# The first block of attention values on other PSUM banks and in other weight tiles, and a Newton step with one tensor operand

## The chip, the cores and the metric

The kernel runs on one NeuronCore of a Trainium2 chip. The metric is the device time of one execution in microseconds (us), as the median of several runs. Engines are named as in the profile: PE is TensorE's matmul, PEld its weight load, DVE is VectorE, ACT is ScalarE, POOL is GpSimd, SP is SyncE, which here only issues DMAs.

## What is computed

One step of a one-layer hybrid decoder: 1024 prompt rows and 8 sample rows of width 1024, everything in float32. The input is normalised, projected by one wide matrix, and goes through three branches (A is attention), which a second matrix merges:

```python
def _rms(x, g):
    xf = x.astype(F32)
    y = xf * lax.rsqrt(jnp.mean(xf * xf, axis=-1, keepdims=True) + EPS)
    return (y * g.astype(F32)).astype(x.dtype)
...
    h = _rms(x, norm_g)
    proj = jnp.einsum('bld,dn->bln', h, w_in)
    ...
    aq = _rms(aq.reshape(B, L, H_A, HD_A), qn_g.reshape(H_A, HD_A)) * (HD_A ** -0.5)
    ak = _rms(ak.reshape(B, L, H_A, HD_A), kn_g.reshape(H_A, HD_A))
    av = av.reshape(B, L, H_A, HD_A)
```

A has 12 heads of width 64 over a mixture of three dilated windows; B is a spatial gating unit, C a gated linear recurrence. The change touches the norm `_rms(x, norm_g)` of the input and the projection `av` of the first four heads.

## The kernel before

The prompt is cut into eight tiles of 128 rows (t = 0 to 7); the 8 sample rows are tile 8. A tile is loaded (`xt`), ACT squares it and sums the squares (`ss`), `rstd` turns the sum into 1/sqrt (a logarithm and an exponential on ACT, then one Newton step on DVE), DVE scales the rows (`xn`), for tiles 3 to 7 POOL multiplies by `norm_g` (2.4 us each), and PE transposes `xn` into PSUM. The result is split into a high and a low half (`h` by ACT, `h` by DVE), and each later product of 128 rows is three matmuls: high by high, high by low, low by high. `hs` holds the transposed sample rows.

`load_w` loads a block of 256 columns of the input matrix as four raw tiles (`wr`, six buffers), rounds each into `wh` (ACT) and takes the rest into `wl` (POOL), four buffers each. Block `qk0` is queries and keys of the first two heads, `v0` values of the first four, `az0` their gates. The four `wh` buffers of `qk0` are free for the next block only when its last product is done.

PSUM has eight banks: `p_proj` two, `p_st` four (scores, and at the start the transposes of `xn`), `p_tr` one, `p_pv` one. `qk_proj` fills the two `p_proj` banks in turn: `pss_qk` (sample rows), then `pqk` 0 to 3, each two row tiles. A `pqk` bank comes free only when ACT has squared it, DVE has summed the squares and made the Newton step, and DVE has written `nat` from it. `v_proj` goes on in the same two banks: `pss_v`, then `pv` 0 to 3. PE transposes `nat` (line 399) into `p_tr`, from where ACT and DVE make the operands of the scores (`KK`, `QQ`, ...).

Attention then works on one head after the other, named by pair and head: scores for the row maximum (`s`), scores again (`st`), exponentials, products with the values (`pv`), and at the end of each half a division, for which `pb` broadcasts the denominators. While PE would wait for ACT and DVE here, projections of later blocks are put between.

The order of all instructions on each engine is made at build time by a scheduler that goes through the program with costs of its own. A small edit can so move rows on every engine. Each engine and each DMA queue then goes through its list in order.

Of the kernel before, what the change touches and what calls it, by code (L numbers as in the profile page):

```python
# [9 lines left out]
F32R = mybir.dt.float32r  # L10
BF16 = mybir.dt.bfloat16
U8 = mybir.dt.uint8
AF = mybir.ActivationFunctionType
ALU = mybir.AluOpType
# [4 lines left out]
P = 128  # L19
D = 1024  # L20
KD = D // P
S = 1024
NT = S // P
# [3 lines left out]
NW = 256  # L27
# [4 lines left out]
EPS = 1e-6  # L32
WB = 2048
OFF_Q, OFF_K, OFF_V, OFF_AZ = 0, 768, 1536, 2304
# [8 lines left out]
N_BIG, N_S2, N_S2B, N_PQ, N_W, N_WL, N_GT, N_RAW, N_E = 16, 6, 2, 5, 4, 4, 2, 6, 3  # L43
# [48 lines left out]
def hybrid_step(tc, ins, outs, parts=("A", "D", "B", "C", "O"), dbg=None):  # L92
    nc = tc.nc
# [8 lines left out]
    with tc.tile_pool(name="const", bufs=1) as cp, tc.tile_pool(name="sb", bufs=1) as sb, \  # L102
            tc.tile_pool(name="ps", bufs=1, space=PSUM) as pm:

        def wk(nm, shape=(P, L), dt=F32):
            return sb.tile(list(shape), dt, tag="big", name=nm, bufs=N_BIG)

        def inp(nm, shape=(P, L), dt=F32):
            return sb.tile(list(shape), dt, tag="big", name=nm, bufs=N_BIG)

        def s2(nm, dt=F32, shape=(P, 512)):
            return sb.tile(list(shape), dt, tag="s2", name=nm, bufs=N_S2)

        def ee(nm, shape=(P, 512), dt=F32):
            return sb.tile(list(shape), dt, tag="e", name=nm, bufs=N_E)
# [4 lines left out]
        def pq(nm, shape=(P, 512), dt=F32):  # L120
            return sb.tile(list(shape), dt, tag="pq", name=nm, bufs=N_PQ)

        def small(nm, n, p=P, dt=F32, bufs=2, tag=None):
            return sb.tile([p, n], dt, tag=tag or f"sm{n}", name=nm, bufs=bufs)

        def psum(tag, nm, bufs, n=512):
            return pm.tile([P, n], F32, tag=tag, name=nm, bufs=bufs)

        def p_proj(nm):
            return psum("proj", nm, 2)  # L130
# [4 lines left out]
        def p_st(nm):  # L135
            return psum("st", nm, 4)
# [21 lines left out]
        def rstd(out, ss, scale, tmp, t2):  # L158

            nc.vector.tensor_scalar(tmp, ss, scale, EPS, ALU.mult, ALU.add)  # L160
            nc.scalar.activation(out, tmp, AF.Ln)
            nc.scalar.activation(out, out, AF.Exp, scale=-0.5)
            nc.vector.tensor_tensor(t2, out, out, ALU.mult)
            nc.vector.scalar_tensor_tensor(tmp, tmp, -0.5, t2, ALU.mult, ALU.mult)
            nc.vector.scalar_tensor_tensor(out, tmp, 1.5, out, ALU.add, ALU.mult)  # L165

        ident = cp.tile([P, P], F32, name="ident")
        nc.scalar.dma_start(ident, ins["ident"])
        ones = cp.tile([P, P], F32, name="ones")
# [9 lines left out]
        qkv_d = tc.dram_tile([4, NS, HA * E], F32, name="qkv_scr")  # L179


        def load_w(cols, nm):
            blk = []
            for i in range(KD // 2):
                hi = sb.tile([P, 2, NW], F32R, tag="whi", name=f"wh_{nm}_{i}", bufs=N_W)
                lo = sb.tile([P, 2, NW], F32R, tag="wlo", name=f"wl_{nm}_{i}", bufs=N_WL)
                raw = sb.tile([P, 2, NW], F32, tag="raw", name=f"wr_{nm}_{i}", bufs=N_RAW)
                o = 0
                for c, w in cols:
                    nc.sync.dma_start(raw[:, :, o:o + w], w_in[:, 2 * i:2 * i + 2, c:c + w])  # L190
                    o += w
                nc.scalar.copy(hi, raw)
                nc.gpsimd.tensor_tensor(lo, raw, hi.bitcast(F32), ALU.subtract)  # L193
                blk.append((hi, lo, raw))
            return blk
# [10 lines left out]
        for t in (0, NT, *range(1, NT)):  # L206
            n = P if t < NT else NS
            xt = inp(f"xt{t}", (P, D))
            nc.sync.dma_start(xt[:n, :], x_p[t * P:(t + 1) * P, :] if t < NT else x_s)
            if t == 1:  # L210
                blk_first = load_w([(OFF_Q, P), (OFF_K, P)], "qk0")
            xn = wk(f"xn{t}", (P, D))
            ss = small(f"ss{t}", 4)
            if t == NT:
                nc.vector.tensor_tensor_reduce(out=xn[:n, :], in0=xt[:n, :], in1=xt[:n, :], op0=ALU.mult, op1=ALU.add,
                                               scale=1.0, scalar=0.0, accum_out=ss[:n, 0:1])
            else:
                nc.scalar.activation(xn, xt, AF.Square, accum_out=ss[:, 0:1])
            rstd(ss[:n, 1:2], ss[:n, 0:1], 1.0 / D, ss[:n, 2:3], ss[:n, 3:4])
            if t in (0, 1, 2, NT):  # L220
                for c in (slice(0, 512), slice(512, D)):
                    nc.vector.scalar_tensor_tensor(xn[:n, c], xt[:n, c], ss[:n, 1:2], g_bc[:n, c], ALU.mult, ALU.mult)
            else:
                nc.vector.tensor_scalar(xn, xt, ss[:, 1:2], None, ALU.mult)
                nc.gpsimd.tensor_tensor(xn, xn, g_bc, ALU.mult)
            for j in range(2):
                ps = p_st(f"tr0_{t}_{j}").rearrange("p (a b) -> p a b", a=4)
                for i in range(4):
                    k = 4 * j + i
                    nc.tensor.transpose(ps[:, i, :n], xn[:n, k * P:(k + 1) * P], ident[:n, :n])  # L230
                hi = h_t[0][j][:, :, t * P:t * P + n]
                lo = h_t[1][j][:, :, t * P:t * P + n]
                nc.scalar.copy(hi, ps[:, :, :n])  # L233
                nc.vector.tensor_tensor(lo, ps[:, :, :n], hi.bitcast(F32), ALU.subtract)
                if t == NT:
                    nc.vector.tensor_copy(hs[:, 4 * j:4 * j + 4, :], ps[:, :, :n])

        def wsl(blk, k, a, b):
            hi, lo, _ = blk[k // 2]
            return hi[:, k % 2, a:b], lo[:, k % 2, a:b]  # L240
# [9 lines left out]
        def rows8(ps, K, i0=0, n=None):  # L250

            n = n or len(K)
            for i, (rows, w) in enumerate(K, i0):
                g = 32 * (i % 4)
                mm(ps[g:g + NS, :NW], rows, w, i < 4, i >= n - 4)

        def add_groups(dst, ps):
            nc.scalar.copy(dst, ps[32:32 + NS, :NW])
            for g in (64, 96, 0):
                nc.vector.tensor_tensor(dst, ps[g:g + NS, :NW], dst, ALU.add)  # L260

        def proj_nat_s(blk, nm):
            ps = p_proj(f"pss_{nm}")
            rows8(ps, [(hs[:, k, :], blk[k // 2][2][:, k % 2, :]) for k in range(KD)])
            dst = small(f"sd_{nm}", NW, NS, tag="sdst")
            add_groups(dst, ps)
            return dst
# [60 lines left out]
        def s_out(n):  # L328
            return outs[n][0, :, 0].rearrange("b h e -> b (h e)")

        VW = 2 * (E + 1)

        def v_proj(sp):
            blk = load_w([(OFF_V + sp * NW, NW)], f"v{sp}")
            st = proj_nat_s(blk, f"v{sp}")
            V = []
            for j in range(2):
                vh = inp(f"vh{sp}_{j}", (P, NT, VW), F32R)
                vl = inp(f"vl{sp}_{j}", (P, NT, P), F32R)
                nc.gpsimd.memset(vh.rearrange("p t (h e) -> p t h e", h=2)[:, :, :, E].bitcast(F32), 1.0)  # L340
                V.append((vh, vl))
            for g in range(4):
                ps = p_proj(f"pv{sp}_{g}").rearrange("p (a b) -> p a b", a=2)
                for j in range(2):
                    proj_nat(blk, 2 * g + j, ps[:, j, :])
                vr = pq(f"vr{sp}_{g}", (P, 2, NW))
                nc.scalar.copy(vr, ps)
                nc.sync.dma_start(new_v[2 * g * P:(2 * g + 2) * P, sp * NW:(sp + 1) * NW]
                                  .rearrange("(a q) c -> q a c", q=P), vr)
                if g < 2:  # L350
                    nc.sync.dma_start(v_d[2 * g * P:(2 * g + 2) * P, sp * NW:(sp + 1) * NW]
                                      .rearrange("(a q) c -> q a c", q=P), vr)
                for j in range(2):
                    vh, vl = V[j]
                    t2 = slice(2 * g, 2 * g + 2)
                    hi = vh[:, t2, :].rearrange("p a (h e) -> p a h e", h=2)[:, :, :, 0:E]
                    src = vr[:, :, j * P:(j + 1) * P].rearrange("p a (h e) -> p a h e", h=2)
                    nc.scalar.copy(hi, src)
                    nc.gpsimd.tensor_tensor(vl[:, t2, :].rearrange("p a (h e) -> p a h e", h=2), src,
                                            hi.bitcast(F32), ALU.subtract)  # L360
            nc.sync.dma_start(qkv_d[2, :, sp * NW:(sp + 1) * NW], st)
            nc.sync.dma_start(s_out("o_vs")[:, sp * NW:(sp + 1) * NW], st)
            return V
# [698 lines left out]
```

## Time and profile before

| | |
|---|---|
| time, median of 3 runs | 1364.37 us (1363.49 to 1366.2) |
| the profiled execution: its time, its span | 1367.91 us, 1366.1 us |
| PE busy | 1277.9 us, 94% of the span |
| DVE, ACT, POOL busy | 914.3, 661.0, 292.6 us |
| mean granted TensorE clock | 0.951 of full |

The span runs from the first instruction to the last of one execution. [...]

### The profile page before, as it was taken

The numbers are of one execution on the slowest core, as the hardware profiler recorded it, in microseconds if no ns is written. First come the engines' busy times: TensorE is split into PE (matmuls) and PEld (weight loads), VectorE is DVE, ScalarE is ACT, GpSimd is POOL, SyncE is SP. The second block draws the span as 40 slices with busy tenths as digits, with TensorE's granted clock in tenths as the row PEclk, the third lists the DMA queues.
The fourth block names the chain that finished last, engine by engine and source line by source line (L and its number), as shares of the span: only waits on it lengthen the run. The fifth ranks groups of instructions, "written<-read, shape, count | busy, mean of one in ns | idle before, by whom it ended". The sixth has DMA issues, their size and how long they took to land. (4 is left out here: it accounts for less than half of the span.)

```text
span 1366.1 us, 27783 instructions
## 1 busy us (share of the span) xinstructions
PE 1277.9 (94%) x10634; PEld 1160.8 (85%) x10634; DVE 914.3 (67%) x2439; ACT 661.0 (48%) x1510; POOL 292.6 (21%) x267
## 2 busy tenths in 40 slices
PE   4799999999889999999999998998899999999999
PEld 3699798779779797898888888987788899899998
DVE  5835775565774656668888988888887623654653
ACT  4435454454443554456654744545544423544543
POOL 2531210131121212112202020211111135311221
PEclk9899899889999799999999999999999999999999
DMA  6241122220221212202433243434253313612210
GB/s 220 42 141 36 47 66 70 59 68 18 58 84 58 76 36 77 65 29 67 119 97 109 90 121 115 111 97 134 61 156 96 92 32 108 207 51 81 74 46 31
DMA packets 165044, 114.23 MB, mean 84 GB/s; under 512 B 13944, under 2 KB 158864, under 8 KB 164912
## 3 DMA queue, kind: packets, MB, share of 16 engines
q1 hardware_dynamic: 157520, 110.28, 27.3%
q10 hardware_dynamic: 6816, 1.54, 0.5%
q8 instruction: 83, 1.36, 0.4%
q0 software_dynamic: 576, 0.64, 0.3%
q14 instruction: 49, 0.40, 0.1%
HBM read 84.60 MB, written 22.09 MB: 78 GB/s over the span
## 5 line engine op out<-in xcount | busy, mean ns | idle before, releaser
L100 PE MATMUL pqk<-wh_qk,h 128*128 128x256 f32 x768 | 159.6, 299 | 5.2 <-ACT h L233 2.8
L100 PE MATMUL pc<-h,wh_cqf 128*128 128x344 f32 x576 | 144.1, 332 | 4.5 <-DVE cz L152 4.5
L100 PE MATMUL po<-woh,yl 128*128 128x256 f32 x512 | 145.0, 284 | 1.9 <-POOL yl L1011 1.9
L100 PE MATMUL po<-woh,yh 128*128 128x256 f32 x512 | 145.7, 285 | 0.0
L100 PE MATMUL po<-wol,yh 128*128 128x256 f32 x512 | 144.4, 282 | 0.0
L100 PEld LDWEIGHTS pqk<-wh_qk,h 128*128 128x128 f32 x768 | 131.5, 204 | 9.8 <-ACT h L233 3.0
L100 PE MATMUL pqk<-wl_qk,h 128*128 128x256 f32 x384 | 114.0, 297 | 0.0
L100 PEld LDWEIGHTS pc<-h,wh_cqf 128*128 128x128 f32 x576 | 102.1, 194 | 7.1 <-DVE cz L152 5.0
L100 PEld LDWEIGHTS po<-woh,yh 128*128 128x128 f32 x512 | 97.1, 190 | 5.6 <-ACT yh L1010 3.9
L100 PEld LDWEIGHTS po<-woh,yl 128*128 128x128 f32 x512 | 97.2, 190 | 4.1 <-POOL yl L1011 2.4
L100 PEld LDWEIGHTS po<-wol,yh 128*128 128x128 f32 x512 | 97.3, 190 | 0.0
L100 PE MATMUL pc<-h,wl_cqf 128*128 128x344 f32 x288 | 94.9, 332 | 2.5 <-POOL wl_cqf L193 2.2
L436 DVE CUSTOM_DVE_ANT_0 s<-s,masks 128x512 f32<-128x512 f32 (+2 forms) x144 | 77.7, 584 | 13.8 <-PE s L100 13.3
L100 PE MATMUL pi<-wh_ci,h 128*128 128x256 f32 x384 | 77.6, 297 | 4.8 <-DVE dsc L925 1.9
L100 PE MATMUL pv<-wh_v,h 128*128 128x256 f32 x384 | 79.1, 297 | 1.9 <-DVE ss L165 1.6
L473 ACT ACTIVATE st<-st 128x512 f32<-128x512 f32 (+2 forms) x84 | 44.2, 536 | 72.9 <-PE st L100 70.2
L100 PEld LDWEIGHTS pqk<-wl_qk,h 128*128 128x128 f32 x384 | 78.1, 204 | 0.5
L100 PE MATMUL pcz<-h,wh_cz 128*128 128x344 f32 x288 | 71.5, 326 | 0.3 <-DVE q L152 0.3
L100 PE MATMUL paz<-h,wh_az 128*128 128x344 f32 x288 | 71.1, 329 | 0.0
L100 PEld LDWEIGHTS pi<-wh_ci,h 128*128 128x128 f32 x384 | 64.2, 201 | 6.9 <-issue 2.9
L1011 DVE TENSOR_TENSOR yl<-yb,yh 128x512 fp32r<-128x512 f32 x44 | 30.4, 692 | 58.0 <-ACT yh L1010 58.0
L100 PEld LDWEIGHTS pv<-wh_v,h 128*128 128x128 f32 x384 | 65.7, 204 | 3.0 <-ACT yo L499 1.8
(376 smaller groups left out, 3665.1 us busy)
## 6 DMA issues: line engine op xcount, KB each, us to landing
wro<-in_w_out_dram SPq DMA_DIRECT2D x32, 256.0 KB
wr_qk<-in_w_in_dram SPq DMA_DIRECT2D x48, 128.0 KB
wr_cqf<-in_w_in_dram SPq DMA_DIRECT2D x48, 128.0 KB
dk<-in_cache_k_dram SPq DMA_DIRECT2D x24, 192.0 KB
dv<-in_cache_v_dram SPq DMA_DIRECT2D x24, 192.0 KB
xt<-in_x_prompt_dram SPq DMA_DIRECT2D x8, 512.0 KB
xr<-in_x_prompt_dram SPq DMA_DIRECT2D x32, 128.0 KB
out_o_yp_dram<-xr SPq DMA_DIRECT2D x32, 128.0 KB
```

The source lines that it names most:

```text
L100: nc.tensor.matmul(out, lhsT=lhsT, rhs=rhs, start=start, stop=stop)
L436: nc.vector.tensor_tensor_reduce(out=ps[:, :w], in0=ps[:, :w], in1=nmask[:, S - n + c:S - n + c + w], op0=ALU.add, op1=ALU.max, scale=1.0, ...
L473: nc.scalar.activation(st[:, :o], st[:, :o], AF.Exp)
L1011: (nc.gpsimd if piece == 0 else nc.vector).tensor_tensor(yl[:, sl, :], y, yh[:, sl, :].bitcast(F32), ALU.subtract)
```

## The change

It has three parts. The values' block `v0` is loaded ahead of the projections into tiles that lie idle until the attention (`s2`, `e`), so it no longer waits for the buffers of `qk0`. Its products go to the four `p_st` banks. And the norm of the input takes `rstd_rows`, which has the same steps as `rstd` with instructions that read one tensor and per-row scalars, and tile 8's squares move from DVE to ACT.

```diff
+        def rstd_rows(out, ss, scale, tmp, t2):
+            nc.vector.tensor_scalar(tmp, ss, scale, EPS, ALU.mult, ALU.add)
+            nc.scalar.activation(out, tmp, AF.Ln)
+            nc.scalar.activation(out, out, AF.Exp, scale=-0.5)
+            nc.vector.tensor_scalar(t2, out, out, tmp, ALU.mult, ALU.mult)
+            nc.vector.tensor_scalar(t2, t2, -0.5, 1.5, ALU.mult, ALU.add)
+            nc.vector.tensor_scalar(out, t2, out, None, ALU.mult)
...
-        def load_w(cols, nm):
+        def load_w(cols, nm, spare=False):
...
+                if spare:
+                    hi = s2(f"wh_{nm}_{i}", F32R, (P, 2, NW))
+                    lo = s2(f"wl_{nm}_{i}", F32R, (P, 2, NW)) if i < 2 else ee(f"wl_{nm}_{i}", (P, 2, NW), F32R)
...
-            if t == NT:
-                nc.vector.tensor_tensor_reduce(out=xn[:n, :], in0=xt[:n, :], in1=xt[:n, :], op0=ALU.mult, op1=ALU.add,
-                                               scale=1.0, scalar=0.0, accum_out=ss[:n, 0:1])
-            else:
-                nc.scalar.activation(xn, xt, AF.Square, accum_out=ss[:, 0:1])
-            rstd(ss[:n, 1:2], ss[:n, 0:1], 1.0 / D, ss[:n, 2:3], ss[:n, 3:4])
+            nc.scalar.activation(xn[:n, :], xt[:n, :], AF.Square, accum_out=ss[:n, 0:1])
+            rstd_rows(ss[:n, 1:2], ss[:n, 0:1], 1.0 / D, ss[:n, 2:3], ss[:n, 3:4])
...
+        blk_v = load_w([(OFF_V, NW)], "v0", True)
...
-            ps = p_proj(f"pss_{nm}")
+            ps = (bank or p_proj)(f"pss_{nm}")
...
-            blk = load_w([(OFF_V + sp * NW, NW)], f"v{sp}")
-            st = proj_nat_s(blk, f"v{sp}")
+            blk = load_w([(OFF_V + sp * NW, NW)], f"v{sp}") if sp else blk_v
+            bank = p_proj if sp else p_st
+            st = proj_nat_s(blk, f"v{sp}", bank)
...
-                ps = p_proj(f"pv{sp}_{g}").rearrange("p (a b) -> p a b", a=2)
+                ps = bank(f"pv{sp}_{g}").rearrange("p (a b) -> p a b", a=2)
```

Line numbers of the changed kernel are 9 to 13 higher behind the new function. Three places show what the scheduler makes of it.

The first is PE at the passage from keys to values, before (`pqk_3` is the last product of queries and keys, `tr_1_0` and `tr_1_1` are transposes of `nat` in the one `p_tr` bank):

```order
L100 MATMUL pqk_3_587<-wh_qk_3_165,h_83 128x256
L399 MATMUL tr_1_0_678<-ident,nat_0_396 128x128 x2
L100 MATMUL pss_v_758<-wr_v_0_736,hs 8x256 x2
L100 MATMUL pss_v_758<-wr_v_1_742,hs 8x256 x2
L100 MATMUL pss_v_758<-wr_v_2_748,hs 8x256 x2
L100 MATMUL pss_v_758<-wr_v_3_754,hs 8x256 x2
L399 MATMUL tr_1_1_689<-ident,nat_1_397 128x128 x2
L100 MATMUL pv_0_778<-wh_v_0_734,h_80 128x256
```

The same place of the change:

```order
L100 MATMUL pqk_3_611<-wl_qk_3_166,h_81 128x256
L100 MATMUL pqk_3_611<-wh_qk_3_165,h_83 128x256
L100 MATMUL pss_v_758<-wr_v_2_373,hs 8x256 x2
L100 MATMUL pss_v_758<-wr_v_3_379,hs 8x256 x2
L100 MATMUL pv_0_778<-wh_v_0_359,h_80 128x256
L100 MATMUL pv_0_778<-wl_v_0_360,h_80 128x256
```

The two transposes have moved away: the second half of `tr_1_0` stands ahead of `pqk_3`, and `tr_1_1` follows only 22 products of `pv_0` later; the other half of `pss_v` lies within `pqk_3`.

The second place is ACT and DVE in the input's norm, while tiles 3 and 4 are prepared. ACT in the change (`wh_v` are the values' weights, `qkg`, `gn`, `lb` small vectors that before were loaded behind the last `h` of tile 7):

```order
L227 ACTIVATE xn_226,ss_227<-xt_224 128x1024
L205 CAST wh_v_2_371<-wr_v_2_373 128x512
L205 CAST wh_v_3_377<-wr_v_3_379 128x512
L295 DMA qkg<-in_q_norm_g_dram 128x6x1
L170 ACTIVATE ss_227<-ss_227 128x1
L296 DMA qkg<-in_k_norm_g_dram 128x6x1
L171 ACTIVATE ss_227<-ss_227 128x1
L227 ACTIVATE xn_253,ss_254<-xt_251 128x1024
L542 DMA gn<-in_hgrn_norm_g_dram 128x6x1
L242 CAST h_80<-tr_1_0_183 128x4x128
L242 CAST h_81<-tr_1_1_190 128x4x128
L546 DMA lb<-in_hgrn_lb_logits_dram 128x6x1
```

And DVE in the change, at the same time:

```order
L169 TENSOR_SCALAR ss_227<-ss_227 128x1
L322 TENSOR_SCALAR qkg<-qkg 128x6
L172 TENSOR_SCALAR ss_227<-ss_227 128x1
L173 TENSOR_SCALAR ss_227<-ss_227 128x1
L174 TENSOR_SCALAR ss_227<-ss_227 128x1
L233 TENSOR_SCALAR xn_226<-xt_224,ss_227 128x1024
L169 TENSOR_SCALAR ss_254<-ss_254 128x1
L243 TENSOR_TENSOR h_82<-tr_1_0_183,h_80 128x4x128
```

The scaling of `qkg` (line 311 before) has moved from behind all of tile 7 to ahead of tile 3's Newton step, and the low half of tile 1's `h` stands behind both.

The third place is PE in the attention, at the first `pb` of head 1 of pair 0. Before:

```order
L100 MATMUL pqk_1_2462<-wh_qk_0_2353,h_80 128x256
L100 MATMUL pqk_1_2462<-wl_qk_0_2354,h_80 128x256
L100 MATMUL pqk_1_2462<-wh_qk_0_2353,h_82 128x256
L100 MATMUL pqk_1_2462<-wh_qk_0_2353,h_80 128x256
L100 MATMUL pb_1_0_1507<-yo_1_0_1502,ones 64x512
L100 MATMUL st_1_1_0_1512<-QQ_1_674,KK_1_672 128x512
```

The same `pb` in the change:

```order
L100 MATMUL pv_1_0_1460<-pl_1_0_1_1478,vh_0_772 65x384
L100 MATMUL pv_1_0_1460<-ph_1_0_2_1496,vh_0_772 65x256
L100 MATMUL pv_1_0_1460<-ph_1_0_2_1496,vl_0_773 64x256
L100 MATMUL pv_1_0_1460<-pl_1_0_2_1493,vh_0_772 65x256
L100 MATMUL pb_1_0_1507<-yo_1_0_1502,ones 64x512
L100 MATMUL st_1_1_0_1512<-QQ_1_698,KK_1_696 128x512
```

Projections stand no longer between the last product with the values and `pb`. Counted over PE's whole list, five `pb` follow their `pv` directly in either program: before, both of head 1 of pair 1 and the second of head 1 of pairs 2, 3 and 4; in the change, both of head 1 of pair 0 and the second of head 1 of pairs 1, 3 and 4. From the last head's first scores on, some 40% into PE's list, the two lists are nearly the same.

## Rows read from the trace of the kernel before

**Rows 1.** The page, part 1: busy time of PE and its share.

```profile
PE 1277.9 (94%) x10634; PEld 1160.8 (85%) x10634; DVE 914.3 (67%) x2439; ACT 661.0 (48%) x1510; POOL 292.6 (21%) x267
```

**Rows 2.** Waits of PE, whole span: us in total, times, longest.

```profile
PE pb L100 <- ACT yo L500: 12.5, 5, 3.2
...
PE pqk L100 <- DVE ss L164: 2.0, 1, 2.0
```

**Rows 3.** Timeline of PE, 59 to 79 us: start, length, instruction, [idle before].

```profile
59.25 0.38 PE L399 MATMUL tr<-ident,nat 128*128 128x128 f32 x2
63.57 1.90 PE L100 MATMUL pss_v<-wr_v,hs 128*8 128x256 f32 x16 [3.94 <-issue]
67.56 0.66 PE L399 MATMUL tr<-ident,nat 128*128 128x128 f32 x2 [2.09 <-DVE KK L414]
68.53 0.55 PE L100 MATMUL pv<-wh_v,h 128*128 128x256 f32 x1 [0.31 <-DVE ss L164]
...
71.66 0.48 PE L100 MATMUL pv<-wh_v,h 128*128 128x256 f32 x2
...
78.02 0.40 PE L100 MATMUL pv<-wh_v,h 128*128 128x256 f32 x2
...
78.38 0.40 PE L100 MATMUL pv<-wh_v,h 128*128 128x256 f32 x2
```

**Rows 4.** Windows, 2 us each: busy per engine, granted clock, DMA share, GB/s.

```profile
62.00:64.00 2.00, 0.43 (x8) 0.20 (x12) 1.86 (x3) 0.00 (x0) 1.10 (x2) 0.50 0.00 0
...
72.00:74.00 2.00, 2.00 (x20) 2.00 (x19) 1.27 (x5) 0.62 (x2) 0.00 (x0) 1.00 0.47 124
```

**Rows 5.** Timeline of ACT, 51 to 56 us (ACTq issues a DMA).

```profile
51.75 0.41 ACTq L284 DMA_DIRECT2D qkg<-in_q_norm_g_dram  x1
...
53.80 1.60 ACTq L533 DMA_DIRECT2D lb<-in_hgrn_lb_logits_dram  x1
55.45 0.60 ACT L298 ACTIVATE sq<-pqk 128x512 f32<-128x512 f32 x1 [3.08 <-issue]
```

**Rows 6.** Timeline of DVE, 18 to 63 us.

```profile
18.94 0.14 DVE L163 TENSOR_TENSOR ss<-ss 128x1 f32<-128x1 f32 x1
...
42.22 2.31 DVE L164 SCALAR_TENSOR_TENSOR ss<-ss 128x8 f32<-128x8 f32 x1
...
49.44 0.68 DVE L160 TENSOR_SCALAR ss<-ss 128x8 f32<-128x8 f32 x1
...
55.95 0.17 DVE L311 TENSOR_SCALAR qkg<-qkg 128x6 f32<-128x6 f32 x1 [2.24 <-DMA qkg<-in_q_norm_g_dram]
...
59.00 1.24 DVE L163 TENSOR_TENSOR ss<-ss 128x8 f32<-128x8 f32 x1 [0.23 <-ACT ss L162]
...
62.78 0.69 DVE L303 TENSOR_TENSOR nat<-pqk,ss 128x512 f32<-128x512 f32 x1
```

**Rows 7.** Timeline of POOL, 42 to 63 us.

```profile
42.13 2.37 POOL L225 TENSOR_TENSOR xn<-xn,g_bc 128x1024 f32<-128x1024 f32 x1 [1.27 <-DVE ss L160]
...
47.70 2.39 POOL L225 TENSOR_TENSOR xn<-xn,g_bc 128x1024 f32<-128x1024 f32 x1 [1.36 <-DVE xn L224]
...
58.93 3.72 POOL L193 TENSOR_TENSOR wl_v<-wr_v,wh_v 128x512 fp32r<-128x512 f32 x3 [5.60 <-ACT wh_v L192]
```

**Rows 8.** Timeline of ACT and PE, 28 to 31 us.

```profile
28.01 1.06 ACT L218 ACTIVATE xn<-xt 128x1024 f32<-128x1024 f32 x1 [4.35 <-DMA xt<-in_x_prompt_dram]
...
30.93 0.79 PE L100 MATMUL pqk<-wh_qk,h 128*128 128x256 f32 x2 [0.22 <-DVE h L234]
```

**Rows 9.** Timeline of PE in the attention, 263 to 282 us.

```profile
263.25 1.96 PE L100 MATMUL pb<-yo,ones 1*64 1x512 f32 x2 [2.49 <-ACT yo L500]
...
280.31 1.96 PE L100 MATMUL pb<-yo,ones 1*64 1x512 f32 x2 [3.21 <-ACT yo L500]
```

**Rows 10.** Windows of the attention, columns as in rows 4.

```profile
158.00:172.00 14.00, 11.04 (x56) 8.22 (x49) 12.22 (x33) 6.52 (x16) 3.61 (x4) 0.76 0.42 126
262.00:288.00 26.00, 21.00 (x80) 15.67 (x81) 17.16 (x38) 15.70 (x33) 6.97 (x12) 0.61 0.20 52
```

More of the change, by code (lines that the diff above doesn't have):

```diff
@@ L179, in hybrid_step @@
         qkv_d = tc.dram_tile([4, NS, HA * E], F32, name="qkv_scr")
-        def load_w(cols, nm):
+        def load_w(cols, nm, spare=False):
             blk = []
             for i in range(KD // 2):
-                hi = sb.tile([P, 2, NW], F32R, tag="whi", name=f"wh_{nm}_{i}", bufs=N_W)
-                lo = sb.tile([P, 2, NW], F32R, tag="wlo", name=f"wl_{nm}_{i}", bufs=N_WL)
+                if spare:
+                    hi = s2(f"wh_{nm}_{i}", F32R, (P, 2, NW))
+                    lo = s2(f"wl_{nm}_{i}", F32R, (P, 2, NW)) if i < 2 else ee(f"wl_{nm}_{i}", (P, 2, NW), F32R)
+                else:
+                    hi = sb.tile([P, 2, NW], F32R, tag="whi", name=f"wh_{nm}_{i}", bufs=N_W)
+                    lo = sb.tile([P, 2, NW], F32R, tag="wlo", name=f"wl_{nm}_{i}", bufs=N_WL)
                 raw = sb.tile([P, 2, NW], F32, tag="raw", name=f"wr_{nm}_{i}", bufs=N_RAW)
@@ L260, in add_groups, with proj_nat_s @@
                 nc.vector.tensor_tensor(dst, ps[g:g + NS, :NW], dst, ALU.add)
-        def proj_nat_s(blk, nm):
-            ps = p_proj(f"pss_{nm}")
+        def proj_nat_s(blk, nm, bank=None):
+            ps = (bank or p_proj)(f"pss_{nm}")
             rows8(ps, [(hs[:, k, :], blk[k // 2][2][:, k % 2, :]) for k in range(KD)])
```

## Prediction

> **What bounds the kernel.** I read the busy times first: PE works for 94% of the span [rows 1], so no other engine can be the bound, and what can be won is PE's idle time and the stretches in which it runs at half clock. Then PE's waits: the largest in the attention are five waits of `pb` for ACT, 12.5 us in all [rows 2]. Then PE's timeline, for the stage that the change touches. From the `nat` transposes at 59.25 to the pair of `pv` matmuls at 71.66 PE is three times idle (3.94, 2.09, 0.31 us), and does little [rows 3]; the windows show the granted clock at 0.50 from 62 us and back at 1.00 at 72 us [rows 4].
>
> Why it waits there: `pss_v` needs the `p_proj` bank of `pqk` 2, which `nat` frees, and `nat` was written at 62.78 to 63.5 [rows 6]. Two things made it late. ACT issued the loads of small vectors before it squared `pqk` 2, and sat idle 3.08 us for that [rows 5]. And the Newton step began at 59.00, just when POOL started three `wl_v` (58.93, 3.72 us) [rows 7]: its first instruction took 1.24 us [rows 6] against 0.14 unhindered at 18.94 [rows 6]. The wait of 2.09 is for the single `p_tr` bank, behind the same `nat`.
>
> **What the change removes.** In the new order `pss_v` and `pv` 0 need no `p_proj` bank, their weights were made 30 us earlier, and the transposes that wait for `p_tr` stand 22 products later. So at that place nothing is left to wait for. The gain: from 59.63 (59.25 + 0.38) to 71.66 is 12.03 us. The same work at full clock: 14 `pv` matmuls (those between 68.53 and 71.66) at 0.12 us, since three of them lie between the starts 78.02 and 78.38 [rows 3], 1.7 us; `pss_v` at half of its 1.90, 0.95; the transposes at about half of 0.66, 0.35. That is 3.0, so 9.0 us fall away, 6.3 idle and 2.7 half clock.
>
> **What it adds at the start.** Every row of the input's norm has moved, so I went through the new lists of ACT, DVE and POOL up to `pv` 0 with the durations of the trace.
>
> Four casts and four `wl_v` (3.72/3 = 1.24 us each) now lie on ACT and POOL before tile 3. POOL had nothing else there, and tile 3's transposes come late enough; I cost them at nothing. If tile 3 were needed at once it would be the 5 us of POOL.
>
> DVE now scales `qkg` ahead of tile 3's Newton step, and so waits for a load of 768 single elements. Before, it was issued at 51.75 and used at 55.95: 4.2 us [rows 5, 6], with few other transfers. Now it is issued at about 25 us, behind the casts of `wh_v`, while the input still loads: ACT waited until 28.01 for tile 4 [rows 8]. With 4.2 us it lands at 29.3, with half as much again at 31.4. Before, PE had the low half of tile 1's `h` at 30.93 [rows 8]. I take 30.5 for DVE's start: then come Newton step and scaling of tile 3 (1.4 us) and that low half (0.7 us, as `nat`), so PE has it at 32.7, 1.8 us later. Bounds: 0 and 4.
>
> Next is the first `nat`, for which PE waited 2.0 us [rows 2]. Before, two Newton steps were held up by POOL's product of a tile: 2.31 us for the instruction at 42.22, under POOL's 42.13 to 44.50 [rows 6, 7]. The rows' own steps no longer wait, but those of `ss` with 8 columns keep `rstd`, and one of them still meets a product of POOL. I find 0.7 us of waiting in place of 2.0: 1.3 back. Net at that point: 0.5 us late; I take 0.7.
>
> The second `nat` is new. Its transpose now stands before `pqk` 3 instead of behind it, and in DVE's list the scaling of tile 7 stands two rows before the Newton step's end. POOL starts on tile 7 (2.39 us [rows 7]) and holds the last instruction of the step. PE has finished `pqk` 2 about 1.5 us before. Bounds: 0 and 2.4; I take 1.5.
>
> Sum up to the values: -9.0 + 0.7 + 1.5 = -6.8 us.
>
> **What moves in the attention.** The gates' projection now runs without scores between it, the first head uses the next keys' projection as filler, and all of A is ahead by about that much. The work is the same and lists agree again at 40%, so only the waits count. Uncovered `pb` are five in both orders. The pair of head 1 of pair 1 (2.49 and 3.21 idle [rows 9]) goes to head 1 of pair 0. That stretch cost 26.0 - 21.0 = 5.0 idle and 21.0 x 0.39 = 8.2 in clock; what head 1 of pair 0 pays so far, 3.0 idle and 11.0 x 0.24 = 2.6, is the lesser kind [rows 10]. So pair 0 loses 7.6, and pair 1, which gets a single uncovered `pb` (about 5.7 by the lesser kind), gains 7.5; in pair 2 one uncovered `pb` (2 to 3 us) is gone; against that, the scores of pairs 2 and 4 stand with less filler (1 to 2 each) and the last but one `pb` of pair 3 with half of its. I take 1.5 us lost, between -4 and +6, for each half-clock stretch of some 5 us that comes or goes is 2.5.
>
> **Sum.** -6.8 + 1.5 = -5.3 us: 1367.91 becomes 1362.6. The profiled execution lies 3.5 above the median of the runs shown, so the median becomes 1359.1.
>
> [...] The row steps lose their second tensor operand. That a tensor operand alone does not decide it is shown by the scaling of 8 columns at 49.44: one tensor, 0.68 us, ending as POOL ends (47.70 + 2.39) [rows 6, 7]. [...] No row shows a one-column step inside a POOL instruction.
>
> **Rivals.** First, more is won: the small vectors land early and the second `nat` is covered (2.2 us), and the attention loses a few half-clock stretches: -9 - 3 = -12, 1352.5. For it: most waits that I find are near zero by my own working. Against: the attention has no more filler than before.
>
> Second, no change: the front's gain is given back by the first tiles. It decides if `qkg` lands after 34 us, 4 us more than I take: then tile 3 and with it POOL's row of products is late, the first `nat` waits 2 us as before, and 6.8 falls to about 2; with the attention's 1.5, 1363.9. For it: the queue of 768 elements in the busiest part of the loads. Against: it took 4.2 us before, and would have to take 9.
>
> Third, slower: head 1 of pair 0 takes over the dear stretch (+7.6) while pair 1 keeps as much as it has, since PE drops to half clock there anyway. It decides when the attention loses more than 6.8 + 2.7 = 9.5 us; 7.6 and the thinner scores of pairs 2 and 4 (3 us) are 10.6, so 1364.4 - 6.8 + 10.6 = 1368.2. Against: pair 1's new order is that of pair 3 before.
>
> Fourth, the Newton step is held up all the same: two holds of about 1.3 us are back on the way to the first `nat`: -5.3 + 2.6, 1361.7, at the edge of no change.
>
> **Numbers.** A measurement of this kernel can tell 0.2%, 2.7 us, from no change. Chances: forecast 0.48, more won 0.13, no change 0.17, slower 0.12, fourth 0.10 (half of it faster by over 0.2%). Of the forecast's 0.48, 0.03 falls short of 0.2%; of the second rival's 0.17, 0.02 is slower by more. Faster 0.63, same 0.23, slower 0.14. Range: the likeliest case alone is 1354 to 1363; down to the first rival's 1352.5 and up past the second, 1353 to 1367 leaves out about 2 in 10.
>
> **What would show it.** After: no idle time of PE over 1 us and a clock of 1.00 between `pqk` 3 and the first `pv`; `pv` 0 starting at 62 to 64 us instead of 68.5; one-column Newton steps of 0.2 us under a POOL product; DVE idle until about 30 for `qkg`; a wait of some 1.5 us at the second pair of `nat` transposes; `pb` waits of 2.5 and 3.2 in head 1 of pair 0. I am wrong if `pv` 0 starts after 66, or if idle time and half clock between 110 and 620 us grow by more than 6.

## The result, and the profile after

The changed kernel takes 1359.26 us, median of 9 runs (1350.77 to 1361.84), beside 1365.17 for the kernel before in the same measurement (1362.7 to 1367.75): ratio 0.9947, 95% interval 0.9925 to 0.9969. Measured once more in the experiments it took 1360.31 us, ratio 0.9971 (0.9954 to 0.9988). The prediction was 1359.1. So the time came out as forecast; the steps did in part, and the experiments show that the parts of the change do not add up the way the prediction took for granted. That the hit is so close is partly luck; the section on the prediction says where.

The span of the profiled execution fell from 1366.1 to 1360.0 us. PE's timeline of the changed kernel, from tile 1 to the first values (the rows that answer to [rows 3, 8]):

```profile
31.17 0.39 PE L100 MATMUL pqk<-wh_qk,h 128*128 128x256 f32 x1 [1.59 <-ACT h L242]
34.21 0.50 PE L100 MATMUL pqk<-wh_qk,h 128*128 128x256 f32 x2 [2.54 <-DVE h L243]
...
47.66 0.44 PE L412 MATMUL tr<-ident,nat 128*128 128x128 f32 x2 [1.45 <-DVE nat L314]
...
56.10 0.44 PE L412 MATMUL tr<-ident,nat 128*128 128x128 f32 x2 [0.52 <-DVE nat L314]
...
60.43 0.62 PE L100 MATMUL pss_v<-wr_v,hs 128*8 128x256 f32 x8
...
64.33 0.39 PE L100 MATMUL pv<-wh_v,h 128*128 128x256 f32 x1
...
88.41 0.28 PE L100 MATMUL pv<-wh_v,h 128*128 128x256 f32 x1
```

A bracket at a row's end is idle time ahead of it; from 56.54 on there is none up to the last row shown. The stall of [rows 3] is gone, and `pv` 0 starts at 64.33 instead of 68.53. The last row is the last `pv` of the first pair. Every order studied here has the same rows, in some order, up to that one, so its start is the bar for the start of the program; I call it the front. Before it is:

```profile
93.82 0.29 PE L100 MATMUL pv<-wh_v,h 128*128 128x256 f32 x1
```

The front is 5.4 us shorter. Two builds with the same order of PE up to there, measured below, differ by 0.9 us in their fronts, and the repeat of the changed kernel by 0.2, so differences under about 1 us say nothing. At the first `pi` row behind the attention, which stands in both orders among the same neighbours, the lead is 684.50 - 680.40 = 4.1 us, and at the end 6.1. In the repeat of the changed kernel the three leads are 5.2, 5.5 and 7.3.

DVE's timeline of the changed kernel (answers to [rows 6]):

```profile
10.52 0.27 DVE L172 TENSOR_SCALAR ss<-ss 128x1 f32<-128x1 f32 x1 [1.10 <-ACT ss L171]
10.83 0.15 DVE L173 TENSOR_SCALAR ss<-ss 128x1 f32<-128x1 f32 x1
...
31.91 0.17 DVE L322 TENSOR_SCALAR qkg<-qkg 128x6 f32<-128x6 f32 x1 [6.81 <-DMA qkg<-in_q_norm_g_dram]
...
39.91 0.27 DVE L172 TENSOR_SCALAR ss<-ss 128x1 f32<-128x1 f32 x1
40.09 1.74 DVE L552 TENSOR_SCALAR lb<-lb 128x6 f32<-128x6 f32 x1
...
44.37 2.30 DVE L164 SCALAR_TENSOR_TENSOR ss<-ss 128x8 f32<-128x8 f32 x1
```

and POOL's beside it (answers to [rows 7]):

```profile
9.82 4.18 POOL L206 TENSOR_TENSOR wl_qk<-wr_qk,wh_qk 128x512 fp32r<-128x512 f32 x3 [1.44 <-ACT wh_qk L205]
...
39.40 2.40 POOL L234 TENSOR_TENSOR xn<-xn,g_bc 128x1024 f32<-128x1024 f32 x1 [3.43 <-DVE lb L551]
44.27 2.38 POOL L234 TENSOR_TENSOR xn<-xn,g_bc 128x1024 f32<-128x1024 f32 x1 [2.47 <-DVE ss L163]
```

Lay one over the other: the one-column steps of L172 and L173 run inside POOL's instructions and take 0.15 to 0.27 us. The 128x6 step at 40.09 ends as POOL ends (41.8), and so does the 128x8 step at 44.37 (46.65). And DVE stood still for 6.81 us, waiting for `qkg`. The change has a price at the start that the prediction did not list: tile 8's square now runs on ACT, and PE waits 3.69 us for that tile's transposes (3.0 in the repeat) and begins the first products at 22.03 instead of 20.14. PE then waits at tile 1 in either kernel (2.81 us before, 1.59 and 2.54 here), which takes this up.

In the attention, PE's wait of `pb` for ACT (answers to [rows 2]) and two of its rows (to [rows 9]), first the waits, then the timeline:

```profile
PE pb L100 <- ACT yo L513: 17.6, 7, 4.3
```

```profile
177.60 1.11 PE L100 MATMUL pb<-yo,ones 1*64 1x512 f32 x2 [2.49 <-ACT yo L513]
...
191.91 1.76 PE L100 MATMUL pb<-yo,ones 1*64 1x512 f32 x2 [2.49 <-ACT yo L513]
```

and the windows of head 1 of pair 0 and of pair 1 (columns as in [rows 4], answers to [rows 10]):

```profile
174.00:200.00 26.00, 20.27 (x99) 15.55 (x98) 18.25 (x39) 13.77 (x25) 0.84 (x2) 0.74 0.23 61
...
262.00:288.00 26.00, 22.58 (x122) 18.84 (x122) 19.36 (x43) 17.47 (x37) 6.99 (x12) 0.87 0.24 66
```

The dear stretch has moved as forecast. Pair 1's window now costs 3.4 us of idle time and 22.58 x 0.13 = 2.9 of clock, where it cost 5.0 and 8.2; pair 0 pays 5.7 and 20.27 x 0.26 = 5.3. Pair 0's window is 26 us long here and was 14 before, with other rows in it, so that comparison is rough.

### The profile page after: what moved, and what is told of

Same layout as the page of the kernel before. It is cut to its first block, busy times and chain, and to the rows that moved or that the text cites. A ratio compares the mean times of both kernels' runs of the same rounds, so it can differ in the third digit from the quotient of the medians.

```text
span 1360.0 us, 27792 instructions
## 1 busy us (share of the span) xinstructions
PE 1271.4 (93%) x10634; PEld 1156.7 (85%) x10634; DVE 909.3 (67%) x2437; ACT 660.7 (49%) x1512; POOL 295.6 (22%) x267
## 3 DMA queue, kind: packets, MB, share of 16 engines
q10 hardware_dynamic: 6816, 1.54, 0.6%
## 5 line engine op out<-in xcount | busy, mean ns | idle before, releaser
L100 PE MATMUL pv<-wh_v,h 128*128 128x256 f32 x384 | 74.4, 289 | 2.2 <-ACT yo L512 2.2
L100 PEld LDWEIGHTS pv<-wh_v,h 128*128 128x128 f32 x384 | 62.8, 196 | 3.7 <-ACT yo L512 2.4
```

Source lines behind the costliest of these rows:

```text
L100: nc.tensor.matmul(out, lhsT=lhsT, rhs=rhs, start=start, stop=stop)
```

## Experiments

The change has three parts: the Newton step (N), the banks (B) and the early weights (W). Single parts and pairs were measured against the kernel before, and variants of the whole. A build-time scheduler sets the order of all rows, and most edits of the front moved rows in the attention and behind it too. So each kernel has two results: the start of the last `pv` of the first pair in its profile, which tells what the edit did to the front, and the time, which holds the new order behind it as well. Expectations that speak of "85 us of work" mean the moment, soon after that row, by which PE had done so much work at full clock.

| kernel | last `pv` (before 93.82) | median us | ratio (95%) |
|---|---|---|---|
| N | 90.03, -3.8 | 1350.23 | 0.9886 (0.9866 to 0.9907) |
| N, scratch columns strided | 89.13, -4.7 | 1351.75 | 0.9905 (0.9887 to 0.9923) |
| B, `pss_v` and `pv` 0 | 87.01, -6.8 | 1350.52 | 0.9894 (0.9875 to 0.9914) |
| W | 95.31, +1.5 | 1369.12 | 1.0039 (1.0025 to 1.0052) |
| N + B, `pss_v` and `pv` 0 | 84.46, -9.4 | 1355.83 | 0.9938 (0.9915 to 0.9961) |
| N + B, all | 84.01, -9.8 | 1361.27 | 0.9968 (0.9952 to 0.9984) |
| N + B, `pv` 0 to 3 | 83.70, -10.1 | 1348.63 | 0.9879 (0.9856 to 0.9901) |
| N + W | 90.31, -3.5 | 1378.54 | 1.0088 (1.0064 to 1.0111) |
| B + W | 92.67, -1.2 | 1362.08 | 0.9987 (0.9967 to 1.0008) |
| N + B + W (the change) | 88.41, -5.4 | 1359.26 | 0.9947 (0.9925 to 0.9969) |
| the same again | 88.62, -5.2 | 1360.31 | 0.9971 (0.9954 to 0.9988) |
| the change, `qkg` scaled late | 90.69, -3.1 | 1360.40 | 0.9961 (0.9941 to 0.9982) |
| the change, `qkg` and `lb` late | 85.68, -8.1 | 1359.88 | 0.9958 (0.9940 to 0.9975) |

**The Newton step alone.** In the kernel before:

```
-            rstd(ss[:n, 1:2], ss[:n, 0:1], 1.0 / D, ss[:n, 2:3], ss[:n, 3:4])
+            rstd_rows(ss[:n, 1:2], ss[:n, 0:1], 1.0 / D, ss[:n, 2:3], ss[:n, 3:4])
```

and the small tile's square on ACT. 

> The kernel before with only the norm's Newton step in the new form (one tensor operand; the small tile's square on ACT). In its order the attention stands as before, the values' first product stands inside the last keys' and queries' product, still in a p_proj bank. Front theory (the gain is the stall at the values' bank, and the Newton form only frees some steps): the bank wait of pss_v stays in some form, 1 to 4 us gained, ratio 0.997 to 0.999, profile about 1362 to 1365 beside 1366. Rival, Newton theory (the freed steps are what brought the 5.9 us): ratio 0.9947 as the whole change.

Measured: 0.9886, more than either theory gave, and 14 us under before. Its front is 3.8 us shorter, so the front theory holds for the front, and the other 10 us lie behind it. In PE's timeline `pss_v` now comes without a wait, in the middle of `pqk` 3, and one of the two large waits is left, for the single `p_tr` bank (it answers to the 2.09 of [rows 3]):

```profile
57.64 1.05 PE L100 MATMUL pss_v<-wr_v,hs 128*8 128x256 f32 x16
...
63.72 0.66 PE L404 MATMUL tr<-ident,nat 128*128 128x128 f32 x2 [3.63 <-DVE KK L419]
```

**Banks and Newton step, weights late.** The changed kernel without the early `load_w`:

```
-        blk_v = load_w([(OFF_V, NW)], "v0", True)
...
-            blk = load_w([(OFF_V + sp * NW, NW)], f"v{sp}") if sp else blk_v
+            blk = load_w([(OFF_V + sp * NW, NW)], f"v{sp}")
```

> The change without its early weights: the values' products in the banks of scores and the new Newton step, but the weights loaded, cast and split where they were before. qkg's load is late again, the attention's order is that of before. Front theory: PE no longer waits for a bank ahead of the values, but wl_v is made by POOL just then (1.24 us a piece): some 1 to 3 us of waiting instead of 6.3, and nothing is lost at 34 us: -5 to -7 us, ratio 0.995 to 0.996. Rival (bank and weights are needed together): PE waits for the weights as long as it waited for the bank: ratio 0.998 to 1.000. Attention theory (the attention's new order costs the 4.6 us of idle time seen there): -9 us or more, ratio under 0.9935.

Measured: 0.9968. The front is 9.8 us shorter, 4.4 more than with the early weights, and no wait is left at the values: late weights cost nothing there, for PE takes the pieces of `pv` 0 to 2 in turn as POOL hands them over. But the order behind the attention is another one, and its price shows in the windows of 620 to 900 us, this kernel first, then the changed kernel:

```profile
620.00:900.00 280.00, 249.12 (x2712) 228.11 (x2711) 235.49 (x679) 148.60 (x351) 49.35 (x44) 0.93 0.37 103
```

```profile
620.00:900.00 280.00, 265.74 (x2799) 243.27 (x2797) 246.85 (x711) 160.44 (x382) 52.16 (x47) 0.98 0.38 106
```

PE is busy 16.6 us less in these 280, and at a lower granted clock (0.93 beside 0.98). No theory had that in it.

**Early weights and Newton step, without the banks.**

```
-            bank = p_proj if sp else p_st
+            bank = p_proj
```

> The change without its banks: early weights in the idle tiles and the new Newton step, but the values' products in p_proj. qkg's load is early and DVE waits for it, and the attention's order is that of after. Front theory: pss_v waits for the nat of the last but one product as before, and the wait for qkg (3 us) is paid as well: between -2 and +3 us, ratio 0.9985 to 1.002. Rival (the weights bring it, the bank not): ratio 0.995.

Measured: 1.0088, 14 us slower. The front gains 3.5, no more than the Newton step alone; behind the attention stands much the order of the run above (PE busy 249.36 of the 280 us there). The ratio is outside both theories. By the front alone, early weights without the banks bring nothing over N.

**One row moved: `qkg` scaled late.** In the changed kernel:

```
-                nc.vector.tensor_scalar_mul(qkg[:, 0, :], qkg[:, 0, :], E ** -0.5)
+                tc.keep_in_program_order(nc.vector.tensor_scalar_mul(qkg[:, 0, :], qkg[:, 0, :], E ** -0.5))
```

> The changed kernel with one row of DVE moved: the scaling of qkg stands behind the last nat of the first pair, where its load has long landed; PE's order is the same to the row. Theory (DVE's wait of 6.81 us for that load is what made the third matmul of tile 1 late, 34.21 instead of 30.93): that matmul is back at 31 to 32 us, PE waits 2.5 us less there and runs some 3 us less at half clock: 2.5 to 4.5 us under the changed kernel, some 1355 to 1357 us, ratio to the kernel before 0.992 to 0.993. Rival (something else is late there anyway, the input's tiles 3 and 4 or POOL's products): the wait moves on to another row and the time stays at that of the changed kernel, 0.9947.

Measured: 0.9961, the rival's answer. The third matmul of tile 1 is back at 31.28, as the theory said, but the wait came back at the next small vector. In ACT's timeline `lb` is issued early too, and DVE now waits for that, 10.3 us from the start of its issue to its use, with tile 4's Newton step queued behind it:

```profile
29.38 0.69 ACTq L546 DMA_DIRECT2D lb<-in_hgrn_lb_logits_dram  x1
```

```profile
39.68 0.17 DVE L547 TENSOR_TENSOR lb<-lb 128x6 f32<-128x6 f32 x1 [5.63 <-DMA lb<-in_hgrn_lb_logits_dram]
```

```profile
40.68 0.55 PE L100 MATMUL pqk<-wh_qk,h 128*128 128x256 f32 x1 [4.14 <-DVE ss L173]
```

Why these loads went early at all can be read from the code. Each is pinned behind the last ACT instruction written before it. That was tile 7's cast; since the early `load_w` stands between, it is the cast of `wh_v` 3, which runs at 25 us. With them went not one load but all: `qkg`, `gn`, `lb`, `dcnt`.

**Both small vectors late.** The same, and the first step on `lb` pinned behind tile 7's rows on DVE:

```
+        tc.keep_in_program_order(nc.vector.tensor_tensor(lb, lb, lb, ALU.subtract))
```

> The changed kernel with the scaling of qkg and the first step on lb pinned late on DVE, so that DVE waits for no load of a small vector while tiles 3 to 7 come in; the loads themselves are issued where they were. The attention's order is nearly that of the changed kernel. Theory (these waits are the whole difference of 5 us that the changed kernel's start has against the run with banks alone): no wait of DVE over 2 us between 24 and 40 us, PE's idle time up to the values 4 us less than in the changed kernel and no half clock there: -10 to -12 at 110 us against before, ratio 0.990 to 0.993. Rival (with the early weights the tiles 4 to 7 themselves arrive late, and PE waits for them): the start stays at -6, ratio 0.9947 or above.

Measured: the front is 8.1 us shorter and has no half clock (mean granted clock up to 110 us: 1.00), 2.7 better than the changed kernel and 1.7 short of N + B: the theory, for the larger part of the difference. PE's rows show the rest. Up to the front it is idle 21.9 us here and 20.1 in N + B, and the largest wait that N + B does not have is 1.87 us, at 30.74, for ACT's `h` of tile 1. In ACT's list its first piece stands behind the square of tile 4, which starts at 29.07, when its load has come in; in N + B that piece runs ahead of the square, at 26.06. So the 1.7 us lie for the most part in the order that the scheduler gave ACT. The time did not follow: 0.9958, where 0.993 was the theory's upper end. The order of the attention is not quite that of the changed kernel either, so this does not say whether the front's gain is lost or paid for by the order.

**`pss_v` and `pv` 0 alone in the banks of scores.**

```
-                ps = bank(f"pv{sp}_{g}").rearrange("p (a b) -> p a b", a=2)
+                ps = (bank if g < 1 else p_proj)(f"pv{sp}_{g}").rearrange("p (a b) -> p a b", a=2)
```

on N + B. 

> As the run with banks alone, but only pss_v and pv 0 in the banks of scores, pv 1 to 3 in p_proj. In this order PE's rows from the second pair on are those of before, row by row, so the attention and all behind it can't differ by their order. Theory (the start's gain is passed on whole): -10 to -12 us at 110 us as with the banks alone, and -10 to -12 at the end, ratio 0.991 to 0.993. Rival (what the start gains is given back, since the waits of the attention are for DVE, ACT and transfers that have not become earlier): -6 or less, ratio 0.9955 or above.

This is the clean one: from the second pair on PE's rows are those of before. Front -9.4; `pi` row at 673.15, -11.4; median 1355.83 beside 1365.14, -9.3 (by the ratio -8.5, with an interval from -5.3 to -11.6). Within the noise the front's gain reaches the end whole. The ratio, 0.9938, lies just above the theory's 0.991 to 0.993, and below the rival's.

**The old Newton step in the changed kernel** (B + W). 

> The changed kernel with the Newton step of the input's norm as it was before (two tensor operands, the small tile's square on DVE). Theory (steps with two tensor operands are held for the rest of POOL's 2.4 us product, one-column steps with one tensor operand aren't): several 128x1 steps of 1 us and more under POOL's products, PE 2 to 4 us later at 85 us of work than in the changed kernel, ratio about 0.997. Rival (the new form brings nothing where DVE waits for qkg anyway): no difference at that point, 0.9947. The attention's order differs in its second and third pair, which may add some us of either sign.

Measured: the last `pv` comes 4.3 us later than in the changed kernel, just beyond the theory's 2 to 4; ratio 0.9987, not told from no change. DVE's timeline shows the first tile's step held three times by POOL's `wl_qk` (9.44 to 14.13) and `wl_v` behind it:

```profile
11.71 1.20 DVE L163 TENSOR_TENSOR ss<-ss 128x1 f32<-128x1 f32 x1
...
12.95 1.19 DVE L164 SCALAR_TENSOR_TENSOR ss<-ss 128x1 f32<-128x1 f32 x1
14.18 1.19 DVE L165 SCALAR_TENSOR_TENSOR ss<-ss 128x1 f32<-128x1 f32 x1
```

The other one-column steps of 8 to 18 us took 0.14 to 0.15 us. PE's first transposes start at 17.22 here and at 12.97 in the changed kernel, but these 4.3 us are not the 4.3 of the front: in the changed kernel PE then waits for tile 8, and `pss_qk` starts at 21.16 here and at 20.96 there. The loss comes later, at two waits of PE:

```profile
34.54 0.58 PE L100 MATMUL pqk<-wh_qk,h 128*128 128x256 f32 x1 [5.80 <-ACT h L246]
...
51.13 0.44 PE L416 MATMUL tr<-ident,nat 128*128 128x128 f32 x2 [3.95 <-DVE ss L160]
```

The changed kernel has 1.59 and 2.54 at the first place and 1.45 at the second. The first is ACT's order: it issues `lb` ahead of tile 1's `h`, and that takes 3.75 us:

```profile
30.10 3.75 ACTq L550 DMA_DIRECT2D lb<-in_hgrn_lb_logits_dram  x1
...
33.90 1.56 ACT L246 CAST h<-tr 128x512 fp32r<-128x512 f32 x3 [3.10 <-issue]
```

The second is the Newton step of `ss` with 8 columns, which is `rstd` in either kernel. Here two of its steps meet two products of POOL in a row (43.13 to 48.34):

```profile
43.70 2.36 DVE L163 TENSOR_TENSOR ss<-ss 128x8 f32<-128x8 f32 x1
46.10 2.27 DVE L164 SCALAR_TENSOR_TENSOR ss<-ss 128x8 f32<-128x8 f32 x1
```

So this run does not isolate the form of the one-column steps. N makes the front 3.8 us shorter on the kernel before (4.7 strided), 2.6 with the bank, 5.0 with the early weights and 4.3 with both; in each pair the order ahead of the front differs too, and tile 8's square moves with N.

**The changed kernel again.** 

> The changed kernel once more, as the bar for the others on this chip and for the spread of its profile: ratio 0.9925 to 0.997; PE's idle time and half-clock loss up to 110 us within 1 us of the first profile (23.7 and 1.7), in the attention within some us of it.

 Measured 0.9971, and a front of 88.62; its leads stand with the result. Up to 110 us PE's idle time and half clock are within 1 us of the first profile, as expected.

**The bank alone**: `pss_v` and `pv` 0 in the banks of scores, all else as before.

```
-            st = proj_nat_s(blk, f"v{sp}")
+            st = proj_nat_s(blk, f"v{sp}", bank)
```

with the `bank` of the run above. 

> The kernel before with one part alone: pss_v and pv 0 in the banks of scores; the Newton step as before, the weights loaded where they were. PE's rows from the second pair on are those of before. Bank theory (the prediction's 9.0 us: the bank is what PE waited for at 60 to 72 us): PE reaches 85 us of work 7 to 9 us before the kernel before, ratio 0.993 to 0.995. Rival (the parts need each other, as the run with the old Newton step showed for bank and weights together, -0.6): with the Newton step still held the nat transposes and the products' weights are as late, and no more than 3 us are won, ratio 0.998.

 Measured: front -6.8, just short of the theory's 7 to 9; time 0.9894, better than either theory. PE's rows are those of before from the third pair on only, not from the second as expected. In PE's timeline the values follow the `nat` transpose with no idle time, where [rows 3] had 6.3 us of it:

```profile
61.66 0.38 PE L414 MATMUL tr<-ident,nat 128*128 128x128 f32 x2
61.97 1.04 PE L100 MATMUL pss_v<-wr_v,hs 128*8 128x256 f32 x14
62.94 0.50 PE L100 MATMUL pv<-wh_v,h 128*128 128x256 f32 x2
```

From there to the last `pv` this build needs 25.35 us (61.66 to 87.01), before 34.57 (59.25 to 93.82): 9.2 less, beside the 9.0 predicted. The front gains only 6.8 because the transposes start 2.4 later: the first transpose of all comes at 15.91 instead of 15.14, and the wait for the first `nat` is 3.50 us instead of 2.04.

**Strided scratch columns**, on N alone; every engine has the same rows in the same order. Only what the steps write is strided; the sums that the first one reads lie side by side as before. In N that first step, L160, with one tensor operand and 8 columns, took 0.62 us at 37.84 and 0.59 at 62.19 and ended with POOL's product; the question is whether the stride frees it.

```
-                rstd(ss[:, 8:16], ss[:, 0:8], 1.0 / E, ss[:, 16:24], ss[:, 0:8])
+                rstd(ss[:, 8:24:2], ss[:, 0:8], 1.0 / E, ss[:, 9:24:2], ss[:, 0:8])
```

> The kernel with the new Newton step alone once more, with one thing changed: in the keys' and queries' rstd the scratch columns for the result and the first step's output lie at every second element instead of side by side; all engines have the same rows in the same order. [...] Rival (it is the number of columns that holds it): L160 still ends with POOL. The time stays that of the Newton step alone, 0.9886 (0.9866 to 0.9907), by either, which makes it a second measurement of that kernel.

 Measured: the rival's answer. L160 on DVE still ends with POOL's instruction (37.66 and 37.63):

```profile
37.04 0.62 DVE L160 TENSOR_SCALAR ss<-ss 128x8 f32<-128x8 f32 x1
```

```profile
35.23 2.40 POOL L230 TENSOR_TENSOR xn<-xn,g_bc 128x1024 f32<-128x1024 f32 x1 [6.24 <-DVE ss L173]
```

**The early weights alone.** 

> The kernel before with only the early weights in the idle tiles: Newton step as before, values' products in p_proj. Theory (the early weights bring the small vectors' loads forward with them, and DVE waits for them): a wait of DVE of 6 us and more for qkg between 24 and 34 us, PE 3 to 6 us later than before at 20 us of work, and no gain at the values, since the bank is still waited for: 0 to +6 us at 85 us of work, ratio 1.000 to 1.005 plus what the attention's other order does. Rival (early weights take a wait off the values): -3 us at 85.

 Measured: 1.0039, slower; front +1.5, with a wait of DVE of 7.27 us for `qkg` (issued at 26.18, used at 32.68). The theory's range; the third matmul of tile 1 comes at 34.43, and ACT's issue of `lb` takes 3.27 us ahead of that tile's `h`.

**`pv` 0 to 3 in the banks of scores, `pss_v` not**, on N + B:

```
-            st = proj_nat_s(blk, f"v{sp}", bank)
+            st = proj_nat_s(blk, f"v{sp}")
```

> As the run with the banks and the new Newton step, weights late, but pss_v in p_proj and only pv 0 to 3 in the banks of scores. By its order PE's rows behind the attention are those of before (not those of the banks run, which lost 22 us there), and between rows 2400 and 3200 (the later pairs) they are mostly those of the kernel with the Newton step alone. Theory (the start's gain is additive, and what lies behind it depends on which order the build came to): -7 to -11 at 85 us of work, no loss between 620 and 900 us, and 14 to 20 us in all, ratio 0.986 to 0.990, better than each part alone. Rival (start's gains don't reach the end): no better than the banks in p_st with the order of before, 0.994.

 Measured: 1348.63 us, 0.9879 (0.9856 to 0.9901): the theory's range, and the lowest median of all, some 11 us under the changed kernel. It is not told from N alone or B alone (their intervals overlap), though its front is 3 to 6 us shorter than theirs.

## Why the prediction was right, and where it wasn't

**The removed stall, -9.0: right.** After has no idle time and a granted clock of 1.00 between the `nat` transposes and the values (54 to 68 us), and B alone takes 9.2 us less from those transposes to the last `pv`.

**The start, +0.7 and +1.5: mis-sized.** It cost 9.0 - 5.4 = 3.6 us instead of 2.2, and `pv` 0 starts at 64.33, just past the 62 to 64 that I gave. The step that failed is the load of `qkg`: taken as 4.2 us or half as much again, so that DVE starts at 30.5; it took 6.2 us (issued at 25.74, used at 31.91; 6.6 in the repeat), and the third matmul of tile 1 came at 34.21 instead of 32.7, 3.3 us later than before where 1.8 was worked out. The second `nat` wait was smaller than worked out (0.52, not 1.5), the first larger (1.45, not 0.7). That the other small vectors had moved with `qkg` stands in the order shown ahead of the prediction (`gn` and `lb` in ACT's list), but no use of `lb` was priced: in the changed kernel DVE waits 0.39 us for it, and 5.63 once `qkg` is out of the way. That tile 8's square on ACT delays its transposes (a wait of 3.69 us) was not priced either; the wait at tile 1 took it up.

**The early weights at nothing: wrong.** Added to N + B they cost 4.4 us in the front (-9.8 against -5.4); with the two waits for small vectors out of the way 1.7 are left (-8.1), most of it ACT's later `h` of tile 1. And what they were to save, a wait of PE for late weights, is not there without them.

**The Newton step: right in kind, its size not isolated.** The fourth rival priced two held steps on the way to the first `nat` at 2.6 us. The run with the old step loses 4.3 in the front, but at waits that the order on ACT and the 8-column steps make. The one-column steps that are held there (1.19 to 1.20 us) are the first tile's, which the prediction passed over; by the start of `pss_qk` they have cost 0.2 us.

That the row steps are held all the same did not come true. That one column goes free was my assumption, taken without a row that shows it; the changed kernel's trace does show it. A one-column Newton step with one tensor operand goes free under POOL (0.15 to 0.27 us, as without it); one with two is held (1.19 to 1.20 with the old step); and steps that read 6 or 8 columns are held with one operand too (1.74 at 40.09; 0.62 even with a stride of two in what is written). Why one column passes was not shown.

**The attention, +1.5: right, by terms that cancel.** From the last `pv` to the first `pi` row it lost 1.3 us, and won 0.3 in the repeat. The exchange between pair 0 (+7.6) and pair 1 (-7.5) measures about +5.4 (5.7 + 5.3 less the 5.6 of [rows 10]; rough, since the windows differ) and -6.9. "Five uncovered `pb` in both orders" is right for the lists, but PE waits at seven in the changed kernel, 17.6 us instead of 12.5: two with little filler ahead of them wait too (1.61 and 1.54).

**The sum, -5.3:** the profile says -6.1, the medians -5.9 and -4.8. How near it came is partly luck: the front gained 5.4 instead of 6.8, the lead at the first `pi` row is 4.1, and 2.0 of the 6.1 arise behind that row, where both lists hold the same rows and nothing was forecast. The nine runs of the changed kernel lie 11 us apart.

What stays open is why one order of the attention is worth so much more than another. N alone and B alone, with fronts 3.8 and 6.8 us shorter, end 14 and 13 us sooner; B alone has before's rows from the third pair on. Most of what they gain beyond the front lies between it and the first `pi` row: that stretch takes 580.9 us in N and 585.6 in B, 590.7 before and 592.0 in the changed kernel. Part of it can be read from PE's wait of `pb` for ACT. N has three, 5.5 us in all, before five with 12.5. That is not the whole: B + W has seven such waits, 16.1 us, and still takes only 584.7. In comparing profiles one has to allow for the profiled execution of before, which lay 3.5 us above its median; builds with the same rows behind the first `pi` row gain 1.6 to 5.3 us there.

## What to carry to other kernels

Where a scheduler orders the program, read what an edit did to the whole order, and measure the parts apart: here each of two parts alone beat the three together by some 9 us. A load that is pinned behind "the instruction before it" moves with whatever is written in between, so look for every small load that an early step drags forward, and let no engine whose next rows are needed soon use such a vector while the large loads run: DVE stood still for 6.81 us here. On DVE, Newton steps on one column with one tensor operand passed under POOL's work here (0.15 to 0.27 us); those with two tensors, and steps that read 6 or 8 columns, ended as its instruction ended (1.20 us on one column, up to 2.30 on 8). What such a wait costs is read at the engine that bounds the kernel: 4.3 us at PE's first transposes were 0.2 us at its first products.

## What was not expected of the hardware

POOL is slowed in some of these overlaps as well: the product of `wl_qk` that ran under DVE's 8x1024 square of tile 8, which has two tensor inputs, took 2.24 us before and 2.25 with the old Newton step in the changed kernel, where an undisturbed one takes 1.26; the product over the held 128x1 steps took 1.26 all the same. A load of 768 single elements took 6.2 us (`qkg` in the changed kernel) to 10.3 us (`lb` with `qkg` scaled late) from issue to use where it was issued early, while the inputs and weights came in; issued late, before, it took 4.2 us (`qkg`) and 3.7 (`lb`). Issuing such a load (`lb`) kept ACT's queue for 0.69 to 3.75 us. In the changed kernel a one-column `TENSOR_SCALAR` takes 0.15 us with two constants, 0.21 with one scalar from a tile and 0.27 with two (L173, L174, L172).
